# A hyena, mLSTM and S5 block on one core: the S5 output tables move from the first stage to the scan, the late modulation takes one k and 1024 columns per operation

## The chip, the cores and the metric

The kernel runs on one NeuronCore of a Trainium2 chip. The time is the device time of one execution in microseconds (us); the figure for the kernel before is the median of three runs.

## The reference

One layer of a hybrid diffusion block on 256 latent tokens that follow 256 context tokens, 2048 channels wide, all in fp32. An adaLN modulation is made from `c` and `c_ctx` (a 2048 x 12288 product). The modulated tokens go through one input projection (2048 x 12304), whose columns feed three branches of 768 channels: a two-step Hyena long convolution, a bidirectional mLSTM and a bidirectional S5 state space model. Each branch is projected to 2048, multiplied with a sigmoid gate per channel (also columns of the input projection), the sum goes through an output projection, a norm and a squared-ReLU MLP of width 8192.

```python
def token_mixer(h_ctx, h_lat, rows, need_ctx, w_in, hy_p, ml_p, s5_p, out_p):
    ...
    ys_c, sst_f, sst_b = s5_bidir(u_c, disc, c_re, c_im, zs, zs, need_ctx)
    ys_l, _, _ = s5_bidir(u_l, disc, c_re, c_im, sst_f, sst_b, True)
    y_lat = merge_branches(hyena_branch(hy_l, rows, *hy_p), mlstm_out(hm_l, o_l, ml_norm_g),
                           s5_out(ys_l, u_l, s5_d, glu_w, glu_b), mg_l, *out_p)

def s5_direction(u, ab_re, ab_im, bb_re, bb_im, c_re, c_im, x0, readout):
    ...
    _, _, s_re, s_im = lax.associative_scan(s5_combine, (a_re, a_im, bu_re, bu_im), axis=1)
    ...
    y = (jnp.einsum('blgp,gcp->blgc', s_re, c_re.astype(F32))
         - jnp.einsum('blgp,gcp->blgc', s_im, c_im.astype(F32)))
    return y, final
```

## The kernel before

Every weight matrix is streamed once, in chunks of 128 x 1024 fp32 (512 KB) that `raw` (L196) loads on SP's queue into four buffers `wr`. For fp32 precision each chunk is split in two parts: ACT copies it to `wh` (L190), DVE subtracts to `wl` (L194), and three matmuls per tile (L211) multiply the parts with the split activations. So each chunk costs one ACT and one DVE operation of 128 x 1024 and, with 256 tokens moving, 24 matmuls.

Each engine has one stream of instructions in a fixed order, which a scheduler made from the program's order and priorities; an engine whose next instruction waits holds up all behind it, DMA issues included (SP, ACT and GpSimd, here POOL, issue DMAs). Work other than the chunks is written as generators, *sides*: after each chunk `chunk_done` (L216) advances up to three of them, each by its rate, and `drain` runs one to its end. The stages in `run` (L1407 to L1536):

- *Stage 0* (scope p0a). The first 4096 columns of the modulation: 8 blocks of 16 chunks, each a fp32 matmul (L406), whose sums end in `modc` (L415). After each pair of blocks `h_group` (L427) multiplies and shifts a quarter of the tokens' channels (L435, on DVE) and splits them, and a quarter of the K projection follows (`part`). Beside it, one step per chunk, runs the side `s5_params` (L440: discretised powers of the poles, `pq`, and the scaled input matrix `s5B`) and `s5_tables` (L540).
- `s5_tables` makes, for six channel tiles, products of powers with C (the output tables Q, lines L536 to L538 in `powers`, L525) and with B (the input tables w). Direction 0 is computed on DVE, direction 1 on POOL. Q goes to DRAM as QD (L568) and, by small matmuls (`pk`, L564), becomes the near-diagonal kernel KK; w is transposed and goes to DRAM as WA.
- *pA.* `s5_spread` (L598) rearranges KK into KD by 8 DMAs; a small gate on kT makes it wait for K. Then V, gates, Q, the mLSTM, U (`u_consume`, L600, which writes UD and keeps the latent u in SBUF as `uT`) and O. The rest of the modulation, `mod_late` (L1164), is a side: 16 blocks of 512 columns, 8 loads of two k rows each, one DVE multiply-add of 128 x 512 (L1181) for each k.
- *pB.* Six chunks of the hyena columns, then `s5_inject` (L616: WA and u, loaded on ACT's queue, give the 64 chunk inputs of the state), then the side `s5_scan` (L645): 63 steps that depend on each other, each of four POOL operations of 128 x 96 (L652 to L655). Beside it the remaining hyena chunks and 32 gate chunks (`mg_consume`, which writes gates to DRAM, MG). Then the side `s5_output` (L658), which needs the scan's end and loads QD, KD and UD on ACT's queue, beside 48 more gate chunks, and `s5_glu`.
- *pC.* `hyena` (L1096), the last 16 of 96 gate chunks, the merges, and the tail: output projection, norm, MLP.

`hy_consume` (L1078) convolves three taps on DVE (L741, L743) and writes HX on POOL's queue (L1087, L1094).

## Time and profile before

| | us |
| --- | --- |
| three runs | 2031.83, 2034.3, 2036.18 |
| median | 2034.3 |
| the profiled execution | 2046.25 |
| its span | 2044.3 |

| engine | busy us | share of the span | instructions |
| --- | --- | --- | --- |
| PE | 1885.0 | 92% | 13945 |
| DVE | 1342.6 | 66% | 1842 |
| ACT | 797.7 | 39% | 1079 |
| POOL | 473.4 | 23% | 654 |

The DMA engines moved 455.92 MB in the span, 223 GB/s on average. Busy shares are averages over stages with different limits, so the rows further down are cut by stage: up to 205 us the last `modc` sum, from 634 to 807 us the scan. The times of rows are of the profiled execution, which is 12 us above the median.

### The profile page before, as it was taken

The numbers are of one execution on the slowest core, as the hardware profiler recorded it, in microseconds if no ns is written. First come the engines' busy times: TensorE is split into PE (matmuls) and PEld (weight loads), VectorE is DVE, ScalarE is ACT, GpSimd is POOL, SyncE is SP. The second block draws the span as 40 slices with busy tenths as digits, with TensorE's granted clock in tenths as the row PEclk, the third lists the DMA queues.
The fourth block names the chain that finished last, engine by engine and source line by source line (L and its number), as shares of the span: only waits on it lengthen the run. The fifth ranks groups of instructions, "written<-read, shape, count | busy, mean of one in ns | idle before, by whom it ended". The sixth has DMA issues, their size and how long they took to land.

```text
span 2044.3 us, 34693 instructions
## 1 busy us (share of the span) xinstructions
PE 1885.0 (92%) x13945; PEld 1716.5 (84%) x13945; DVE 1342.6 (66%) x1842; ACT 797.7 (39%) x1079; POOL 473.4 (23%) x654
## 2 busy tenths in 40 slices
PE   4787899999999896999889998899999999999996
PEld 1555888898998896999769977899989899998986
DVE  8789876655876564455777767866655555555556
ACT  1233333324544332534333443544343334444332
POOL 4777311000015997000343400500000000000001
PEclk8898899999999898999999999999999999999998
DMA  8798667766698675777756876577765566666653
GB/s 311 262 299 285 195 203 221 228 199 184 206 318 272 211 242 172 262 251 243 270 183 217 278 249 218 174 248 229 244 208 190 189 185 181 184 185 230 190 187 115
DMA packets 255200, 455.92 MB, mean 223 GB/s; under 512 B 28789, under 2 KB 75541, under 8 KB 253504
## 3 DMA queue, kind: packets, MB, share of 16 engines
q1 hardware_dynamic: 221824, 382.43, 59.0%
q0 software_dynamic: 12384, 44.54, 6.2%
q10 hardware_dynamic: 20832, 26.75, 3.9%
q8 instruction: 109, 1.79, 0.4%
q14 instruction: 51, 0.42, 0.1%
HBM read 424.75 MB, written 32.05 MB: 223 GB/s over the span
## 4 chain that ended last, share of the span: by engine, by line
PE 64%; DVE 14%; DMA 8%; POOL 8%; issue 4%; ACT 1%; ACTq 0%; POOLq 0%; DVEq 0%; SPq 0%
PE mm L211 57%; DMA wr<-in_w_mod_dram 4%; PE aux L211 4%; DVE wl L194 4%; POOL sc L654 2%; POOL sc L653 2%; POOL t L655 2%; POOL sc L652 2%; DVE t L194 1%; DMA wr<-in_w_in_dram 1%; DVE ty L435 1%; ACT wh L190 1%; DVE mac L1181 1%; DVE s5t L537 1%; DMA s5wq<-WA 1%
## 5 line engine op out<-in xcount | busy, mean ns | idle before, releaser
L211 PE MATMUL mm<-t,wh 128*128 128x256 f32 x5888 | 1102.7, 288 | 24.8 <-ACT wh L190 12.6
L211 PEld LDWEIGHTS mm<-t,wh 128*128 128x128 f32 x5888 | 933.7, 194 | 46.6 <-ACT wh L190 13.9
L194 DVE TENSOR_TENSOR wl<-wr,wh 128x1024 fp32r<-128x1024 f32 (+1 forms) x517 | 657.0, 1277 | 381.6 <-ACT wh L190 380.7
L211 PE MATMUL mm<-t,wl 128*128 128x256 f32 x2944 | 850.1, 289 | 23.3 <-DVE wl L194 23.0
L190 ACT ACTIVATE wh<-wr 128x1024 fp32r<-128x1024 f32 (+1 forms) x517 | 546.4, 1058 | 807.9 <-PE mm L211 577.6
L211 PEld LDWEIGHTS mm<-t,wl 128*128 128x128 f32 x2944 | 571.4, 194 | 37.4 <-DVE wl L194 29.4
L1181 DVE SCALAR_TENSOR_TENSOR mac<-wr,vecs,mac 128x512 f32<-128x512 f32 x240 | 186.8, 778 | 152.7 <-DMA wr<-in_w_mod_dram 150.0
L211 PE MATMUL mm<-wh,t 128*128 128x512 f32 (+1 forms) x960 | 249.3, 349 | 1.7 <-ACT wh L190 1.7
L211 PEld LDWEIGHTS mm<-wh,t 128*128 128x128 f32 x960 | 169.7, 191 | 25.6 <-ACT wh L190 2.7
L211 PE MATMUL mm<-wl,t 128*128 128x512 f32 (+1 forms) x480 | 169.2, 352 | 5.2 <-DVE wl L194 5.2
L211 PE MATMUL mm<-wh,ff 128*128 128x512 f32 (+1 forms) x576 | 155.3, 358 | 0.0
L211 PEld LDWEIGHTS mm<-wh,ff 128*128 128x128 f32 x576 | 101.8, 188 | 17.6
L211 PEld LDWEIGHTS mm<-wl,t 128*128 128x128 f32 x480 | 91.6, 191 | 21.7 <-DVE wl L194 10.5
L211 PE MATMUL mm<-wl,ff 128*128 128x512 f32 (+1 forms) x288 | 103.0, 357 | 0.0
L1403 POOL DMA_DIRECT2D t<-in_ln_g_dram x1 | 0.5, 535 | 358.8 <-PE mm L211 358.8
L211 PE MATMUL mm<-ty,wh 128*128 128x256 f32 x384 | 74.1, 291 | 0.0
L211 PE MATMUL mm<-ty,wl 128*128 128x256 f32 x192 | 57.0, 297 | 6.7 <-DVE wl L194 6.7
L211 PEld LDWEIGHTS mm<-ty,wh 128*128 128x128 f32 x384 | 61.6, 195 | 0.9
L211 PEld LDWEIGHTS mm<-wl,ff 128*128 128x128 f32 x288 | 54.2, 188 | 8.8
L1192 POOL DMA_DIRECT2D mrow<-b x8 | 4.0, 502 | 227.8 <-DVE b L1190 227.8
L211 PE MATMUL aux<-t,t 128*128 128x384 f32 (+3 forms) x160 | 48.8, 422 | 8.0 <-DVE t L1147 3.5
L406 PE MATMUL px<-wr,b 128*32 128x512 f32 x128 | 40.3, 714 | 12.9 <-DVE s5t L335 10.7
(389 smaller groups left out, 1813.6 us busy)
## 6 DMA issues: line engine op xcount, KB each, us to landing
wr<-in_w_ff_dram SPq DMA_DIRECT2D x256, 512.0 KB, 3.9
wr<-in_w_in_dram SPq DMA_DIRECT2D x192, 512.0 KB, 4.7
wr<-in_w_mod_dram SPq DMA_DIRECT2D x160, 512.0 KB, 4.8
wr<-in_w_out_dram SPq DMA_DIRECT2D x32, 512.0 KB, 4.9
wh<-in_w_mod_dram SPq DMA_DIRECT2D x16, 512.0 KB, 6.2
wl<-in_w_mod_dram SPq DMA_DIRECT2D x16, 512.0 KB, 7.8
QD<-s5Q POOLq DMA_DIRECT2D x24, 256.0 KB, 4.9
WA<-s5wa ACTq DMA_DIRECT2D x24, 256.0 KB, 5.2
```

The lines of the kernel that those rows point to most:

```text
L190: return self.nc.scalar.activation(out, in_, f, bias=bias, scale=scale)
L194: self.nc.vector.tensor_sub(lo, x, hi.bitcast(F32))
L211: self.nc.tensor.matmul(out, lhsT, rhs, start=start, stop=stop, skip_group_check=True)
L406: nc.tensor.matmul(ps[o:o + 32], self.st[:, k, :], raw[:, kk, :], start=k < 4, stop=k >= KT - 4, skip_group_check=True, tile_position=(0, o))
L435: self.nc.vector.tensor_scalar(h[:, j], h[:, j], self.modc[:, 16 + k, m:m + 1], self.modc[:, k, m:m + 1], op0=ALU.mult, op1=ALU.add)
L537: e.tensor_mul(t[:, :, s], bcp(s), bcm(1))
L652: v.tensor_mul(t1, self.a8[:, 0], S[:, :, :, :, n - 1])
L653: v.tensor_mul(t2, self.a8[:, 1], S[:, :, ::-1, :, n - 1])
L654: v.tensor_add(t1, t1, S[:, :, :, :, n])
L655: v.tensor_add(S[:, :, :, :, n], t1, t2)
L1181: v.scalar_tensor_tensor(acc, x, c, acc, op0=ALU.mult, op1=ALU.add)
L1192: nc.gpsimd.dma_start(self.mrow[which // 3:which // 3 + 1, o:o + 512], brow)
```

## The change

1. `h_group`'s multiply and shift goes from DVE to ACT.
2. `s5_tables` is split. `s5_into` stays in stage 0 and makes the input tables alone, for both directions on DVE and four pairs per operation (128 x 512 and 128 x 1024 elements where there were 128 x 256 and 128 x 512); it saves `s5B` and `pq` to DRAM (SB, PQ). The output tables, `pk`, QD and KK are a side (rate 0.6) in a new scope pT, from the end of the injection on, beside hyena and gate columns; they load SB, PQ and C anew, all products on DVE (128 x 576 and 128 x 1152). QD and KK are written on ACT's queue. `s5_spread` comes at their end, and the gate on K is gone.
3. `s5_inject` starts after four hyena chunks where there were six, and loads WA in 24 pieces of 256 KB, on POOL's queue.
4. `uT` goes through DRAM (UL). `s5_output` loads all it needs on POOL's queue, at rate 0.4 beside 24 gate chunks; 40 gate chunks in place of 16 are left for beside and behind hyena.
5. `mod_late` loads one k and 1024 columns at a time, with one DVE operation of 128 x 1024 for each load, 128 loads of 512 KB as before.
6. The mLSTM's states take four smaller tiles in place of one large one.

```diff
-                    self.nc.vector.tensor_scalar(h[:, j], h[:, j], self.modc[:, 16 + k, m:m + 1],
-                                                 self.modc[:, k, m:m + 1], op0=ALU.mult, op1=ALU.add)
+                    self.act(h[:, j], h[:, j], AF.Identity, bias=self.modc[:, k, m:m + 1],
+                             scale=self.modc[:, 16 + k, m:m + 1])
...
-    def powers(self, out, m, d, q, l0, n):
+    def powers(self, out, m, d, ct, l0, n):
-        e = self.nc.vector if d == 0 else self.nc.gpsimd
-        k = q.stop - q.start
+        v = self.nc.vector
+        q = slice(24 * d + 4 * ct, 24 * d + 4 * ct + 4)
...
         for s in range(2):
-            e.tensor_mul(out[:, :, s], bcp(1 + s), bcm(0))
-            e.tensor_mul(t[:, :, s], bcp(s), bcm(1))
-        e.tensor_add(out, out, t)
+            v.tensor_mul(out[:, s], bcp(1 + s), bcm(0))
+            v.tensor_mul(t[:, s], bcp(s), bcm(1))
+        v.tensor_add(out, out, t)
+
+    def s5_into(self):
+        nc = self.nc
+        for ct in range(CT):
+            wt = []
+            for d in range(2):
+                w = self.t(self.br, [P, 2, 4, P], "s5w", 4)
+                self.powers(w.rearrange("p s q (l c) -> p s q l c", c=16), self.s5B, d, ct, d, LC)
+                wt.append(w)
+            yield
...
     def s5_tables(self):
...
+        nc.gpsimd.dma_start(B.rearrange("p a b c -> p (a b c)"), self.SB)
+        nc.gpsimd.dma_start(self.pq.rearrange("p a b c -> p (a b c)"), self.PQ)
+        nc.gpsimd.dma_start(C, self.I["s5c"])
+        yield
         for ct in range(CT):
...
+            for d in range(2):
+                q = slice(24 * d + 4 * ct, 24 * d + 4 * ct + 4)
+                Q = self.t(self.br, [P, 2, 4, 144], "s5Q", 2)
+                self.powers(Q.rearrange("p s q (l c) -> p s q l c", c=16), C, d, ct, 0, 9)
...
-                    nc.gpsimd.dma_start(self.QD[ct, d, :, 2 * half:2 * half + 2], Q[:, :, :, o:o + P])
+                nc.scalar.dma_start(self.QD[ct, d], Q[:, :, :, o:o + P])
...
+        self.s5_spread()
...
     def s5_inject(self):
...
-            wa = self.t(self.br, [P, 4, 4, P], "s5wq", 2)
-            nc.scalar.dma_start(wa, self.WA[ct])
...
+            for i in range(4):
+                wa = self.t(self.br, [P, 4, P], "s5wa", 4)
+                nc.gpsimd.dma_start(wa, self.WA[ct, :, i])
...
-        for b in range(16):
-            c0 = 2 * D + b * 512
-            acc = self.t(self.sm, [P, 512], "mac", 1)
-            for k0 in range(0, KT, 2):
-                wt = self.raw(w, k0, 2, c0, 512)
...
+        for b in range(8):
+            c0 = 2 * D + b * 1024
+            acc = self.t(self.sm, [P, 1024], "mac", 1)
+            for k in range(KT):
+                x, c = self.raw(w, k, 1, c0, 1024)[:, 0], self.sc[:, k:k + 1]
...
-                    yield from self.s5_tables()
+                    yield from self.s5_into()
...
-            with self.scope("pB") as self.br:
-                self.n6 = 5
-                hy = self.lin_w_steps(w_in, O_HY, 3 * W, KT, lat, self.hy_consume)
-                self.run_steps(hy, 6)
-                self.s5_inject()
+            hy = self.lin_w_steps(w_in, O_HY, 3 * W, KT, lat, self.hy_consume)
+            with self.scope("pT") as self.br:
+                self.run_steps(hy, 4)
+                for _ in self.s5_inject():
+                    pass
                 self.sides[1][1] = 0.3
                 self.with_side(self.s5_scan(), 2)
+                self.with_side(self.s5_tables(), 0.6, 2)
                 self.run_steps(hy, 36)
-                self.run_steps(steps, 32)
-                self.with_side(self.s5_output(), 0.6)
-                self.run_steps(steps, 48)
+                self.run_steps(steps, 24)
+                self.drain(2)
+            with self.scope("pB") as self.br:
+                self.run_steps(steps, 8)
+                self.with_side(self.s5_output(), 0.4)
+                self.run_steps(steps, 24)
                 self.drain()
                 self.s5_glu()
```

How the change moves instructions is shown at three places. First DVE late in stage 0, around two `modc` sums of the kernel before (`s5t` and `s5Q` are the table products, `s5w` the input tables, `ty` sums of K):

```order
L537 TENSOR_TENSOR s5t_31_129<-s5pq_189,s5B_121 128x2x128 x2
L538 TENSOR_TENSOR s5w_1325<-s5w_1325,s5t_31_129 128x512
L537 TENSOR_TENSOR s5t_31_129<-s5pq_189,s5C_122 128x2x144 x2
L536 TENSOR_TENSOR s5w_1470<-s5pq_189,s5B_121 128x2x128 x2
L1460 TENSOR_TENSOR ty_108<-ty_108,mm_1758 128x1024
L590 TENSOR_TENSOR s5kk_1408<-s5kk_1408,aux_1152 128x16
L536 TENSOR_TENSOR s5w_1596<-s5pq_189,s5B_121 128x2x128 x2
L194 TENSOR_TENSOR wl_1843<-wr_1840,wh_1842 128x1024
L415 TENSOR_TENSOR modc_101<-px_1820,vecs_93 128x8
L536 TENSOR_TENSOR s5Q_216_1419<-s5pq_189,s5C_122 128x2x144 x2
```

and DVE at a like place of the kernel after:

```order
L537 TENSOR_TENSOR s5w_722<-s5pq_190,s5B_124 128x512 x2
L194 TENSOR_TENSOR t_23_106<-ty_113,t_23_106 128x512
L539 TENSOR_TENSOR s5w_716<-s5w_716,s5t_130 128x1024
L194 TENSOR_TENSOR wl_979<-wr_976,wh_978 128x1024
L538 TENSOR_TENSOR s5t_130<-s5pq_190,s5B_124 128x512 x2
L539 TENSOR_TENSOR s5w_722<-s5w_722,s5t_130 128x1024
L1476 TENSOR_TENSOR ty_110<-ty_110,mm_899 128x1024
L194 TENSOR_TENSOR wl_1060<-wr_1057,wh_1059 128x1024
L1476 TENSOR_TENSOR ty_111<-ty_111,mm_975 128x1024
L415 TENSOR_TENSOR modc_104<-px_1037,vecs_96 128x8
```

The products with C (`s5Q`, 128x2x144) are gone from the stage; those with B (`s5w`) come in one operation for four pairs, and stand earlier.

Second, POOL late in the scan. Before, the four operations of a step (`sc`, `t`) with a gate write (MG) now and then:

```order
L652 TENSOR_TENSOR sc_850_6418<-t_713_5520 128x96
L653 TENSOR_TENSOR sc_851_6419<-t_713_5520 128x96
L654 TENSOR_TENSOR sc_850_6418<-sc_850_6418,t_713_5520 128x96
L655 TENSOR_TENSOR t_713_5520<-sc_850_6418,sc_851_6419 128x96
L1211 DMA MG_74<-mg_7562 128x512
L652 TENSOR_TENSOR sc_852_6424<-t_713_5520 128x96
L653 TENSOR_TENSOR sc_853_6425<-t_713_5520 128x96
L1211 DMA MG_74<-mg_7565 128x512
L654 TENSOR_TENSOR sc_852_6424<-sc_852_6424,t_713_5520 128x96
```

and after, with hyena writes (HX), gate writes, the eight DMAs of `s5_spread` (KD) and two loads of `s5_output` (QD) inside one step of the scan, whose four lines are L666 to L669 now:

```order
L666 TENSOR_TENSOR sc_901_6359<-t_637_4883 128x96
L667 TENSOR_TENSOR sc_902_6360<-t_637_4883 128x96
L1102 DMA HX_93<-b_999_6937 128x256
L1102 DMA HX_93<-b_1000_6942 128x256
L680 MEMSET b_1146_8192 128x1024
L668 TENSOR_TENSOR sc_901_6359<-sc_901_6359,t_637_4883 128x96
L1224 DMA MG_74<-mg_7545 128x512
L1224 DMA MG_74<-mg_7548 128x512
L611 DMA KD_73<-KK_92 48x16x128 x8
L686 DMA s5wq_8198<-QD_77 128x2x1024
L686 DMA s5wq_8316<-QD_77 128x2x1024
L669 TENSOR_TENSOR t_637_4883<-sc_901_6359,sc_902_6360 128x96
```

All these DMAs now stand in the stream that carries the scan: 37 between its first and its last step, with 10 memsets, where there were 15 and 2.

Third, DVE beside the scan. Before, the splits of the weight chunks (`wl`), the multiply-adds of `mod_late` (`mac`) and the convolution of hyena (`b`):

```order
L1181 SCALAR_TENSOR_TENSOR mac_6472<-wr_7398,vecs_93,mac_6472 128x512
L194 TENSOR_TENSOR wl_7335<-wr_7332,wh_7334 128x1024
L1181 SCALAR_TENSOR_TENSOR mac_6472<-wr_7398,vecs_93,mac_6472 128x512
L194 TENSOR_TENSOR wl_7371<-wr_7368,wh_7370 128x1024
L741 SCALAR_TENSOR_TENSOR b_1008_7279<-b_1007_7277,vecs_93,b_1008_7279 128x4x63
L741 SCALAR_TENSOR_TENSOR b_1009_7284<-b_1007_7277,vecs_93,b_1009_7284 128x4x63
L743 SCALAR_TENSOR_TENSOR b_1008_7279<-b_1007_7277,vecs_93,b_1008_7279 128x4x63
L743 SCALAR_TENSOR_TENSOR b_1009_7284<-b_1007_7277,vecs_93,b_1009_7284 128x4x63
L194 TENSOR_TENSOR wl_7405<-wr_7402,wh_7404 128x1024
```

and after:

```order
L539 TENSOR_TENSOR s5Q_5845<-s5Q_5845,s5t_5320 128x1152
L194 TENSOR_TENSOR wl_6381<-wr_6378,wh_6380 128x1024
L759 SCALAR_TENSOR_TENSOR b_810_5869<-b_806_5857,vecs_96,b_810_5869 128x4x63
L538 TENSOR_TENSOR s5t_5320<-s5pq_5319,s5C_5318 128x576 x2
L194 TENSOR_TENSOR wl_6432<-wr_6429,wh_6431 128x1024
L194 TENSOR_TENSOR wl_6477<-wr_6474,wh_6476 128x1024
L537 TENSOR_TENSOR s5Q_6366<-s5pq_5319,s5C_5318 128x576 x2
L539 TENSOR_TENSOR s5Q_6080<-s5Q_6080,s5t_5320 128x1152
L757 SCALAR_TENSOR_TENSOR b_813_5879<-b_806_5857,vecs_96,b_813_5879 128x4x63
L194 TENSOR_TENSOR wl_6531<-wr_6528,wh_6530 128x1024
L538 TENSOR_TENSOR s5t_5320<-s5pq_5319,s5C_5318 128x576 x2
```

The products and sums of the output tables (`s5Q`, `s5t`) and of KK stand between the splits. From the injection to the first operation that needs the scan's end, DVE has 143 operations where it had 88: 48 splits (44 before), 13 multiply-adds of 1024 (26 of 512), 26 of the convolution (14), 38 table products of 128 x 576 and 10 table sums of 128 x 1152 (none), and small ones.

## Rows read from the trace of the kernel before

**Rows 1.** Windows: length; busy (count) of PE, PEld, DVE, ACT, POOL; clock; DMA; GB/s.

```profile
0.00:40.00 40.00, 19.60 (x82) 4.48 (x82) 32.48 (x134) 5.41 (x18) 11.54 (x30) 0.87 0.95 343
40.00:100.00 60.00, 43.72 (x304) 31.43 (x306) 47.18 (x57) 18.47 (x50) 48.05 (x58) 0.80 0.75 251
100.00:180.00 80.00, 63.12 (x477) 45.50 (x472) 71.08 (x86) 26.17 (x75) 58.00 (x75) 0.89 0.91 298
...
0.00:205.00 205.00, 146.51 (x1024) 95.64 (x1024) 173.37 (x299) 59.20 (x165) 137.57 (x189) 0.88 0.86 290
```

**Rows 2.** DVE's groups to 205 us: xcount | busy us, mean ns | idle us.

```profile
L536 DVE TENSOR_TENSOR s5Q<-s5pq,s5C 128x288 f32<-128x288 f32 x24 | 19.2, 838 | 6.1 <-PE aux L564 6.1
L537 DVE TENSOR_TENSOR s5t<-s5pq,s5C 128x288 f32<-128x288 f32 x24 | 18.9, 822 | 0.2
...
L435 DVE TENSOR_SCALAR ty<-ty,modc 128x256 f32<-128x256 f32 x24 | 16.9, 772 | 0.1
L538 DVE TENSOR_TENSOR s5w<-s5w,s5t 128x512 f32<-128x512 f32 x11 | 16.5, 1498 | 0.3
```

**Rows 3.** POOL's issues of QD in the same stretch, columns as rows 2.

```profile
L568 POOL DMA_DIRECT2D QD<-s5Q x23 | 18.0, 783 | 13.9 <-DVE s5Q L538 11.7 <-POOL s5Q L538 1.8 <-POOL s5bb L554 0.3
```

**Rows 4.** DVE's timeline behind the last modc sum: start us, length us.

```profile
204.99 0.16 DVE L415 TENSOR_TENSOR modc<-px,vecs 128x8 f32<-128x8 f32 x1
205.07 3.12 DVE L537 TENSOR_TENSOR s5t<-s5pq,s5B 128x256 f32<-128x256 f32 x2
208.11 4.63 DVE L435 TENSOR_SCALAR ty<-ty,modc 128x256 f32<-128x256 f32 x8
```

**Rows 5.** ACT's timeline there, one operation of 128 x 256.

```profile
213.62 0.42 ACT L190 ACTIVATE b<-b 128x256 fp32r<-128x256 f32 x1
```

**Rows 6.** Chain of waits where PE runs without a stop: start, length.

```profile
418.37 34.63 PE mm L211 x287
```

**Rows 7.** Window of the scan, columns as rows 1.

```profile
634.00:807.00 173.00, 141.52 (x1118) 138.90 (x1116) 93.74 (x93) 57.08 (x66) 162.62 (x267) 0.92 0.67 216
```

**Rows 8.** Groups in the scan's window, columns as rows 2.

```profile
L194 DVE TENSOR_TENSOR wl<-wr,wh 128x1024 fp32r<-128x1024 f32 x45 | 63.4, 1433 | 20.0 <-ACT wh L190 20.0
L1181 DVE SCALAR_TENSOR_TENSOR mac<-wr,vecs,mac 128x512 f32<-128x512 f32 x26 | 23.8, 914 | 28.9 <-DMA wr<-in_w_mod_dram 28.7
L1211 POOL DMA_DIRECT2D MG<-mg x8 | 4.6, 573 | 0.1
L743 DVE SCALAR_TENSOR_TENSOR b<-b,vecs,b 128x252 f32<-128x252 f32 x7 | 4.4, 657 | 0.0
...
L666 POOL MEMSET b<- 128x1024 f32 x1 | 1.0, 966 | 0.0
```

**Rows 9.** Tile sc, the scan's first operation: ns min/median/max, first to last start us.

```profile
L652 POOL TENSOR_TENSOR sc<-t x63: 433/446/1302, 634.4 to 806.8; 128x96 f32<-128x96 f32 x63
```

**Rows 10.** POOL's timeline at the scan's end: one step to the next.

```profile
799.72 0.43 POOL L652 TENSOR_TENSOR sc<-t 128x96 f32<-128x96 f32 x1
...
801.49 0.44 POOL L652 TENSOR_TENSOR sc<-t 128x96 f32<-128x96 f32 x1
```

**Rows 11.** What PE waited for at L687, the first output matmuls: us, times.

```profile
POOL sc L652: 31.8, 2
```

**Rows 12.** DVE's groups from 300 to 600 us, columns as rows 2.

```profile
L194 DVE TENSOR_TENSOR wl<-wr,wh 128x1024 fp32r<-128x1024 f32 x62 | 75.5, 1221 | 35.8 <-ACT wh L190 35.5
L1181 DVE SCALAR_TENSOR_TENSOR mac<-wr,vecs,mac 128x512 f32<-128x512 f32 x83 | 62.1, 748 | 24.3 <-DMA wr<-in_w_mod_dram 23.1
...
L935 DVE TENSOR_TENSOR DT<-DT,t 128x512 f32<-128x512 f32 x14 | 9.5, 687 | 2.4 <-ACT DT L190 2.3
```

**Rows 13.** Window of hyena, columns as rows 1.

```profile
960.00:1110.00 150.00, 131.56 (x950) 121.18 (x949) 115.79 (x144) 54.74 (x77) 55.08 (x57) 0.95 0.67 222
```

**Rows 14.** DMA issues on the page: KB each, median us to landing.

```profile
s5wq<-WA ACTq DMA_DIRECT2D x6, 1024.0 KB, 10.2
```

More of the change, by code (lines that the diff above doesn't have):

```diff
@@ L445, in s5_params @@
         nc.gpsimd.dma_start(par, I["s5a"])
-        B, C = (self.t(self.br, [P, 2, 48, 16], tag, 1) for tag in ("s5B", "s5C"))
+        B = self.t(self.br, [P, 2, 48, 16], "s5B", 1)
         nc.gpsimd.dma_start(B, I["s5b"])
-        nc.gpsimd.dma_start(C, I["s5c"])
         yield
         are, aim, lg = par[:, 0, :], par[:, 1, :], par[:, 2, :]
-        self.work = [self.t(self.br, [P, 1152], f"s5t{d}", 1) for d in range(2)]
-        tmp = self.slices(self.work[0][:, :1104].rearrange("p (a n) -> p a n", n=48))
+        self.work = self.t(self.br, [P, 1152], "s5t", 1)
+        tmp = self.slices(self.t(self.br, [P, 23, 48], "s5tmp", 1))
         dt_, mag, ph, cs, sn = (tmp(x) for x in ("dt", "mag", "ph", "cs", "sn"))
@@ L503, in s5_params @@
         br, bi = B[:, 0], B[:, 1]
-        w1, w2 = (self.work[1][:, 384 * i:384 * i + 384].rearrange("p (q c) -> p q c", c=16) for i in range(2))
+        w1, w2 = (self.work[:, 384 * i:384 * i + 384].rearrange("p (q c) -> p q c", c=16) for i in range(2))
         for d in range(2):
@@ new lines, in s5_tables @@
+            for d in range(2):
+                q = slice(24 * d + 4 * ct, 24 * d + 4 * ct + 4)
+                Q = self.t(self.br, [P, 2, 4, 144], "s5Q", 2)
+                self.powers(Q.rearrange("p s q (l c) -> p s q l c", c=16), C, d, ct, 0, 9)
+                bb = self.t(self.br, [P, 2, 4, 32], "s5bb", 2)
+                nc.gpsimd.memset(bb, 0.0)
+                for h in range(2):
+                    for s in range(2):
+                        self.act(bb[64 * h:64 * h + 64, s, :, 16 * h:16 * h + 16],
+                                 B[64 * h:64 * h + 64, s, q, :], scale=1.0 - 2.0 * s)
+                yield
+                l0 = 0 if d == 0 else 16
+                for s in range(2):
+                    for p in range(4):
+                        nc.tensor.matmul(pk[32 * p:32 * p + 32, d, :], bb[:, s, p, :], Q[:, s, p, l0:l0 + P],
+                                         start=d == 0 and s == 0, stop=s == 1, skip_group_check=True,
+                                         tile_position=(0, 32 * p))
+                o = 16 - l0
+                nc.scalar.dma_start(self.QD[ct, d], Q[:, :, :, o:o + P])
@@ L687, in s5_output @@
                         self.nc.tensor.matmul(py[o:o + 64, p // 2, :], xb[:, p, d, s].rearrange("p g j -> p (g j)"),
-                                              Q[:, d, p, s, :], start=p < 2 and d == 0 and s == 0, stop=False,
+                                              Q[:, d, s, p, :], start=p < 2 and d == 0 and s == 0, stop=False,
                                               skip_group_check=True, tile_position=(0, o))
@@ L1169, in mod_late @@
         w = self.I["w_mod"][0]
-        for b in range(16):
-            c0 = 2 * D + b * 512
-            acc = self.t(self.sm, [P, 512], "mac", 1)
-            for k0 in range(0, KT, 2):
-                wt = self.raw(w, k0, 2, c0, 512)
-                for kk in range(2):
-                    k = k0 + kk
-                    x, c = wt[:, kk], self.sc[:, k:k + 1]
-                    if k == 0:
-                        v.tensor_scalar(acc, x, c, None, op0=ALU.mult)
-                    else:
-                        v.scalar_tensor_tensor(acc, x, c, acc, op0=ALU.mult, op1=ALU.add)
-                if k0 + 2 < KT:
+        for b in range(8):
[3 more added lines that the diff above has]
+                x, c = self.raw(w, k, 1, c0, 1024)[:, 0], self.sc[:, k:k + 1]
+                if k == 0:
+                    v.tensor_scalar(acc, x, c, None, op0=ALU.mult)
+                else:
+                    v.scalar_tensor_tensor(acc, x, c, acc, op0=ALU.mult, op1=ALU.add)
+                if k + 1 < KT:
@@ L1183, in mod_late @@
                     yield
-            which = b // 4
+            which, o = divmod(b, 2)
+            o *= 1024
             if which in (0, 3):
-                ps = self.aux([1, 512], "px")
-                self.mm(ps, self.ones, acc, True, True)
-                brow = self.b2([1, 512])
-                nc.gpsimd.dma_start(brow, self.I["b_mod"][0:1, c0:c0 + 512])
-                v.tensor_add(brow, brow, ps)
-                o = (b % 4) * 512
-                nc.gpsimd.dma_start(self.mrow[which // 3:which // 3 + 1, o:o + 512], brow)
-            else:
-                ps = self.aux([P, 4], "px")
-                for j in range(4):
+                brow = self.b4([1, 1024])
+                nc.gpsimd.dma_start(brow, self.I["b_mod"][0:1, c0:c0 + 1024])
+                for i in range(0, 1024, 512):
+                    ps = self.aux([1, 512], "px")
+                    self.mm(ps, self.ones, acc[:, i:i + 512], True, True)
+                    v.tensor_add(brow[:, i:i + 512], brow[:, i:i + 512], ps)
+                nc.gpsimd.dma_start(self.mrow[which // 3:which // 3 + 1, o:o + 1024], brow)
+            else:
+                ps = self.aux([P, 8], "px")
+                for j in range(8):
```

126 lines of the change are left out of this document (52 added, 74 removed).

## The prediction, blind

> **What bounds the kernel now.** PE is busy 92% of the span, so what matters is where it is not, and I read the windows by stage first. Up to 205 us PE works 146.5 us of 205; DVE is at 85% and the DMA engines at a share of 0.86 [rows 1]. The stage is bound by weights that must arrive, and held below full DMA pace by DVE, which has the S5 tables between the splits: in the first 40 us, where few tables are made, the share is 0.95, then 0.75 and 0.91. The other large hole is the scan: from 634 to 807 us PE works 141.5 of 173 us [rows 7], and the wait is at its end, where the first output matmuls stood 31.8 us until POOL was done [rows 11]. So the scan's length on POOL sets that stretch.
>
> Why is it so long? At its end, where nothing else runs, a step takes 1.77 us [rows 10], so 63 steps would take 111.5 us. From 634.4 to 806.8 us they take 172.4, and single operations whose median is 446 ns take up to 1302 [rows 9]. 15 DMA issues at 0.57 us [rows 8] and two memsets of about 1 us are 11 of the difference. The other 50 us came beside 93.74 us of busy DVE [rows 7]: each microsecond of DVE work costs the scan 0.53 us. That is my price for everything DVE is given in this stretch.
>
> **The change part by part.** All sums are against the profiled execution (2046.25 us); the forecast is the same difference from the median, 2034.3.
>
> *Stage 0.* Removed: 24 and 24 products with C on DVE at 0.84 and 0.82 us, as many on POOL, and the writes of QD [rows 2, 3]. L435's 24 operations of 0.77 us go to ACT, whose operations of that shape take 0.42 [rows 5] and which is at 29%. Added: DVE makes the input tables of both directions, 24 and 24 products of 512 elements and 12 sums of 1024; at 1.50 us for 512 elements [rows 2] the products are 72 us, half of which DVE had before. DVE thus loses some 40 + 17 us and gains 36, and POOL, which slows it, has nearly nothing left. Bytes: the window moves 290 GB/s x 205 us = 59.4 MB in 176 us of full DMA work (0.86 x 205). QD and C take 6.8 MB with them, of which 1.45 (SB, PQ) and about 1 MB of WA, now all within the stage, come back: 4.4 MB x 2.97 us = 13 us, leaving 163, and I add 3 us for the smaller packets of those writes: 166 us. At which share? Between 0.86 as now (193 us, a gain of 12) and 1.0 (166 us, a gain of 39) I take 0.92, nearest to the 0.91 and 0.95 of the stretches that run well: 180 us, a gain of 25. Behind the last `modc` sum stood 3.12 us of table products and 4.63 us of L435 before the next split [rows 4]; L435 costs ACT 8 x 0.42 = 3.4 us. That gives 5. **Stage 0: -30** (-12 to -46, the upper end with all 7.75 us).
>
> *Start of the scan.* With four hyena chunks ahead in place of six, and side work set otherwise, 120 fewer matmuls of 256 columns stand between V and the scan. At 34.63/287 = 0.1207 us [rows 6]: **-14.5**. They aren't saved, they come later.
>
> *The scan.* DVE work beside it, from the order: 48 splits x 1.433 = 69 us; 13 multiply-adds of 1024, each 0.748 plus 512 elements at the slope of 1221 against 687 ns, 1.28 us, slowed as the splits are (1433 against 1221, x 1.2), 1.54 us, together 20; 26 convolutions x 0.657 = 17 [rows 8, 12]; 38 table products of 576 at 687 ns x 576/512 x 1.2 = 0.93, 35 us; 10 sums of 1152 at 1.6, 16 us; small ones 2. Sum 159 us, x 0.53 = 84. To this 37 DMA issues x 0.6 = 22 us and 10 memsets, 4 us. So 111.5 + 84 + 22 + 4 = 221.5 us against 172.4: **+49**. Lower bound: tables at their free time (43 us, 23 after x 0.53), eight more us for convolutions, issues that hide in gaps: +31. Upper bound: tables at the 1.50 us per 512 elements that products took beside a busy POOL, 87 us, 46 after x 0.53; with 8, 24 for issues and memsets and some 5 where a DMA waits for its data in POOL's stream (KD for the last KK): +83. PE can fill 1188 x 0.1207 = 143 us and some 20 for `pk` and small ones of the 221; it stands about 58 us at the first output matmuls. What would hide the scan's length is more chunks, and those stand behind.
>
> The Trainium skill (SBUF — State Buffer, Who interferes with whom) says that a DVE operation with two SBUF inputs contends with a GpSimd one that reads SBUF, and that the loser blocks for the whole instruction; by it each microsecond of such DVE work would cost the scan one, and the rival of the full lock below is this rule's result. The trace agrees that they contend, but at 0.53 us for each.
>
> *After the scan.* 7890 matmuls where there were 7825: 65 x 0.1207 = **+7.8**. Hyena has 24 more gate chunks to lie beside. PE works 131.6 of 150 us there [rows 13]; I take a quarter of those 18 us back, **-5** (-15 to +5: DVE is at 77% there, and the chunks bring it splits).
>
> *The late modulation.* The same 128 loads; a 1024 operation in place of two of 512 saves the fixed part, 687 - 512 x (1221 - 687)/512 = 0.15 us [rows 12], 18 us of DVE over the 120 pairs. DVE isn't what PE waits for in most of the kernel: **-2** (-4 to 0).
>
> *Injection.* WA comes in 24 pieces through four buffers on POOL's queue: five refills. 1 MB took 10.2 us [rows 14], so 51 us, against 390 matmuls x 0.1207 = 47 us between the first and the last injection. I take 0, bounds 0 to +15 (each refill 3 us late). `uT` through DRAM: six writes on ACT's queue and six loads hidden beside chunks, 0. The mLSTM's four tiles: 0.
>
> **Sum:** -30 - 14.5 + 49 + 7.8 - 5 - 2 = **+5.3, about 2040 us**.
>
> **The rivals.**
>
> *Faster.* Stage 0 runs at full DMA pace and the tables cost the scan little: -44 - 14.5 + 40 + 7.8 - 5 - 2 = -17.7, 2017 us. For it speak the share of 0.95 in the first 40 us and the DVE time that stage 0 loses; against it that the K chunks and DVE's splits stay, and that the share was 0.91 at best later. It decides if the last `modc` sum comes before 172 us and the scan takes under 215. Chance 0.34.
>
> *The loads on POOL's queue bind.* Injection starts 3 us late at each refill, +15: 2055 us. For it: four buffers of 256 KB, a queue that carries other loads. Against: the first four are loaded long before. Chance 0.14.
>
> *A full lock.* Each microsecond of two-input DVE work stops the scan for one: 48 x 1.22 + 13 x 1.28 + 17 + 43 = 135 us at free durations, 111.5 + 135 + 26 = 273 us, +100 in place of +49: 2091 us. Against it: the same count on the scan of before, 45 x 1.22 + 26 x 0.75 + 9 = 84, would make it 206 us, and it took 172.4. Chance 0.06.
>
> *The change doesn't do what it says.* The order shows the tables beside the scan, not behind it: their last sum stands two thirds of the way to the first operation that needs the scan's end. So "beside hyena and gate columns" is beside the scan, which is my forecast itself.
>
> **How the numbers follow.** A measurement can tell about 0.2%, 4 us, from no change. The forecast (0.46) by its own spread, 2024 to 2058, gives slower 0.34, same 0.09, faster 0.03; the faster rival gives faster 0.33 and same 0.01; the queue slower 0.13, same 0.01; the lock slower 0.06. Together faster 0.36, same 0.11, slower 0.53. Below, the range goes to 2006 (all of stage 0 and the scan at +31 give -28.7); above to 2074 (the scan's upper bound, +34 more). What lies outside is the lock and the ends of both cases, under 0.2.
>
> **What would show it right or wrong.** Right: the last `modc` sum at about 180 us; the scan at 215 to 228 us from first to last step, 3.5 us a step; POOL's operations at 0.7 us mean beside DVE; a wait of about 58 us for POOL at the first output matmul; PE's busy time unchanged. Wrong: a scan under 200 us, which would say that products with broadcast inputs cost POOL less than splits do; a `modc` sum still at 195 us, which would say that stage 0 was never held by tables; PE waiting for `s5wa` before the scan.

## The result and the profile after

The changed kernel takes 2056.69 us (four runs, 2049.97 to 2061.03) against 2033.16 for the kernel before (four runs): a ratio of 1.0111 with a 95% interval of 1.0077 to 1.0144, some 23 us slower. A second set of four runs, beside the last experiments, gave 1.0113 (1.0076 to 1.0149). The forecast was 2040 us, slower, with a range of 2006 to 2074.

To see where the time went I cut both traces at the same five places: the last of the 64 gate matmuls that follow V's first chunks, the scan's first step, the first output matmul, the first transpose of x in the tail, the end. First the kernel before, windows by these cuts (columns as in [rows 1]):

```profile
0.00:242.30 242.30, 176.35 (x1250) 123.75 (x1251) 204.99 (x348) 73.97 (x188) 146.93 (x205) 0.87 0.82 274
242.30:634.40 392.10, 387.99 (x3216) 361.05 (x3215) 268.39 (x530) 156.42 (x252) 33.24 (x50) 1.00 0.72 226
634.40:807.60 173.20, 141.12 (x1114) 138.50 (x1113) 93.93 (x92) 57.67 (x68) 163.19 (x268) 0.92 0.67 215
807.60:1280.30 472.70, 439.08 (x3340) 408.37 (x3340) 318.65 (x396) 198.14 (x257) 95.45 (x104) 0.97 0.73 242
1280.30:2044.00 763.70, 740.49 (x5030) 684.79 (x5030) 456.59 (x480) 311.51 (x317) 34.59 (x30) 0.98 0.62 195
```

and the changed kernel, by the same cuts:

```profile
0.00:203.20 203.20, 159.80 (x1058) 113.20 (x1059) 121.38 (x246) 69.15 (x112) 9.17 (x33) 0.88 0.88 300
203.20:600.10 396.90, 379.68 (x3090) 350.31 (x3089) 253.11 (x467) 148.04 (x251) 35.09 (x67) 0.97 0.66 209
600.10:824.00 223.90, 167.11 (x1361) 158.83 (x1360) 146.68 (x145) 73.26 (x126) 203.45 (x298) 0.89 0.70 225
824.00:1300.40 476.40, 442.36 (x3411) 414.57 (x3411) 316.12 (x362) 199.52 (x260) 106.44 (x118) 0.98 0.75 244
1300.40:2057.00 756.60, 736.42 (x5032) 681.24 (x5032) 455.07 (x462) 311.47 (x317) 35.29 (x28) 0.99 0.63 198
```

Read the second number of each line (length) and the third (PE busy). The first cut comes 39.1 us earlier, with DVE busy 121 us where it was 205 and POOL 9 where it was 147. The stretch up to the scan is 4.8 us longer though PE has 8.3 us less to do in it. The scan's stretch is 50.7 us longer, the next 3.7, the tail 7 shorter. PE's work is the same in both (1885 us), so the time is its idle time: 66.0, 4.1, 32.1, 33.6 and 23.2 us before; 43.4, 17.2, 56.8, 34.0 and 20.2 after. Of the scan's 50.7 us, 26.0 are work of PE that now lies there. In idle time stage 0 gives 22.6 us back, and the start of the scan (13.1) and the scan (24.7) take more than that.

These stages sum to +13 us, not to the 23 of the medians: the profiled execution of before lies 12 us above its median, that of the changed kernel 3. A second profile of the kernel before (e8, span 2041.0) has 246.3, 388.7, 175.0, 472.1 and 758.9 us, so a stage of one profile is good to about 5 us. Against the second profile of the changed kernel (e12) the difference is 18.5 us.

Stage 0 ran as the first rival, "Faster", asked (its other condition, a scan under 215 us, was not met): the last `modc` sum came at 170.21 us, where it was 204.99 [rows 4], and the window before it (columns as in [rows 1]) has the DMA share at 0.92, the value that the forecast took:

```profile
0.00:170.00 170.00, 132.58 (x848) 86.69 (x848) 97.36 (x212) 52.59 (x86) 6.96 (x29) 0.89 0.92 315
```

The scan: tile sc in the changed kernel, to be held against [rows 9] (433 ns at the least, 446 at the median; from first to last start 223.0 us where it was 172.4):

```profile
L666 POOL TENSOR_TENSOR sc<-t x63: 428/498/2172, 600.1 to 823.1; 128x96 f32<-128x96 f32 x63
```

DVE's groups beside it, the changed kernel from 600 to 824 us, against [rows 8]:

```profile
L194 DVE TENSOR_TENSOR wl<-wr,wh 128x1024 fp32r<-128x1024 f32 x48 | 64.4, 1346 | 49.8 <-ACT wh L190 47.4 <-PE mm L211 2.2
...
L537 DVE TENSOR_TENSOR s5Q<-s5pq,s5C 128x576 f32<-128x576 f32 x19 | 19.2, 1047 | 3.0 <-PE aux L591 3.0
L1193 DVE SCALAR_TENSOR_TENSOR mac<-wr,vecs,mac 128x1024 f32<-128x1024 f32 x13 | 18.2, 1398 | 4.2 <-DMA wr<-in_w_mod_dram 4.1
L538 DVE TENSOR_TENSOR s5t<-s5pq,s5C 128x576 f32<-128x576 f32 x18 | 18.0, 1037 | 0.0
L539 DVE TENSOR_TENSOR s5Q<-s5Q,s5t 128x1152 f32<-128x1152 f32 x10 | 15.8, 1575 | 0.0
```

The table operations are there, 53 us. But DVE's splits idled 47.4 us for ACT, and the waits of the same stretch (us, times, longest) tell why:

```profile
ACT s5bb L190 <- POOL s5bb L581: 65.4, 8, 12.0
...
PE mm L211 <- ACT wh L190: 25.5, 8, 9.1
...
ACT b L190 <- POOL t L669: 17.1, 1, 17.1
ACT b L190 <- DMA HX<-b: 15.3, 3, 10.6
PEld aux L703 <- POOL sc L666: 14.1, 1, 14.1
...
PE mm L211 <- DVE wl L194: 9.5, 14, 1.6
```

ACT, whose queue also holds the splits `wh`, waited 65.4 us for the eight zeroings of `s5bb` (0.3 us each) that stand in POOL's stream between steps of the scan. So PE was held up along the whole stretch, and at its end only 14 us were left of the 58 us that the forecast put there.

### The profile page after: what moved, and what is told of

Its sections match the earlier page's. It is cut to its first block, busy times and chain, and to the rows that moved or that the text cites. A ratio compares the mean times of both kernels' runs of the same rounds, so it can differ in the third digit from the quotient of the medians.

```text
span 2057.8 us, 34431 instructions
## 1 busy us (share of the span) xinstructions
PE 1885.4 (92%) x13945; PEld 1718.2 (83%) x13945; DVE 1292.4 (63%) x1678; ACT 801.4 (39%) x1062; POOL 389.4 (19%) x540
## 5 line engine op out<-in xcount | busy, mean ns | idle before, releaser
L211 PE MATMUL mm<-t,wh 128*128 128x256 f32 x5888 | 1117.9, 290 | 58.0 <-ACT wh L190 33.6
L194 DVE TENSOR_TENSOR wl<-wr,wh 128x1024 fp32r<-128x1024 f32 x517 | 651.0, 1262 | 488.9 <-ACT wh L190 480.9
L190 ACT ACTIVATE wh<-wr 128x1024 fp32r<-128x1024 f32 x517 | 545.0, 1057 | 804.2 <-PE mm L211 585.5
L1193 DVE SCALAR_TENSOR_TENSOR mac<-wr,vecs,mac 128x1024 f32<-128x1024 f32 x120 | 162.1, 1350 | 114.4 <-DMA wr<-in_w_mod_dram 113.8
L211 PE MATMUL mm<-ty,wh 128*128 128x256 f32 x384 | 68.3, 280 | 0.6 <-ACT wh L190 0.6
```

Source lines behind the costliest of these rows:

```text
L190: return self.nc.scalar.activation(out, in_, f, bias=bias, scale=scale)
L194: self.nc.vector.tensor_sub(lo, x, hi.bitcast(F32))
L211: self.nc.tensor.matmul(out, lhsT, rhs, start=start, stop=stop, skip_group_check=True)
L1193: v.scalar_tensor_tensor(acc, x, c, acc, op0=ALU.mult, op1=ALU.add)
```

## The experiments

Every ratio is to the kernel before, run beside on the same chip. Theory A: the scan's length on POOL, 0.53 us for each us of DVE work, sets the stretch. Later, as A2: PE is starved by ACT, held in POOL's stream; and to remove that is worth something only if there are chunks to put before the scan's end.

**e1.** The zeroing of `s5bb` on DVE.

```diff
-                nc.gpsimd.memset(bb, 0.0)
+                v.memset(bb, 0.0)
```

> The changed kernel with one edit: the zeroing of the small tiles s5bb (L581) is done by DVE, not by POOL. In the changed kernel's trace ACT, whose queue also holds the splits, waited 65.4 us for these eight memsets, which stand in POOL's stream between steps of the scan. Theory A, the scan's own length sets the stretch (224 us from its first step to the first output matmul): the idle time of PE only moves from the middle to the end, the wait for POOL at the first output matmul grows from 14 to about 50 us, the scan stays at 217 to 225 us, and the time stays within 5 us of the changed kernel's, ratio to before 1.008 to 1.013. Rival B, these waits are what is lost: PE gets back most of the 43 us that it idled before the end, the time falls by 20 us or more, ratio about 1.000 or under.

Measured: 2050.14 us, ratio 1.0072 (1.0051 to 1.0093), a little below A's range and the changed kernel's interval, though the two intervals overlap. The scan took 215.5 us. Rival B is out: the waits went, 20 us did not come back. But A was wrong on where the idle time goes. It stayed in the middle, PE standing only 4 us at the output, because the next dependence took over. The waits of e1 from 596.5 to 813 us:

```profile
ACT b L190 <- DMA HX<-b: 50.9, 6, 11.7
```

The buffers of `hy_consume` come free behind the HX writes, which POOL issues, and these too stand between the scan's steps.

**e2.** No products of the output tables (Q one tile of zeros).

```diff
-                Q = self.t(self.br, [P, 2, 4, 144], "s5Q", 2)
-                self.powers(Q.rearrange("p s q (l c) -> p s q l c", c=16), C, d, ct, 0, 9)
+                Q = Q0
```

> The changed kernel without the products of the output tables: Q is one tile of zeros, and the 24 + 24 products of 128 x 576 and 12 sums of 128 x 1152 on DVE are left out (the S5 output then lacks the scan's part); memsets, small matmuls, all DMAs stay. Theory A (0.53 us of scan for each us of DVE work beside it): 53 us of DVE work leave the scan's stretch, which falls by 28 us to about 196 us, and the time by about 25 us, ratio to before about 0.999. Rival C, it is the DMA issues and memsets in POOL's stream that lengthen the scan: the scan stays over 212 us and the time falls by under 10 us, ratio 1.007 or more. A full lock between DVE and POOL would take 45 us or more off the scan.

Measured: 2041.31 us, ratio 1.0025 (1.0007 to 1.0042). The scan took 199.2 us, where A said 196 and C over 212; DVE's work beside it fell from 147.4 to 104.5 us only, since other work filled part of the 53; a full lock, a microsecond for each, would have taken the scan to about 180. The time fell by 15 to 18 us rather than 25; in this profile the stretch before the scan was 10 us longer (407 us). So the products beside the scan are worth most of the 23 us, but without them the kernel is still not faster than before.

**e3.** e1 and sixteen more gate chunks ahead of the output.

```diff
-                self.run_steps(steps, 8)
+                self.run_steps(steps, 24)
                 self.with_side(self.s5_output(), 0.4)
```

> The kernel of e1 (memsets on DVE) and sixteen more gate chunks ahead of the S5 output: 24 + 24 where 24 + 8 stood, so that 24 are left for beside and behind hyena in place of 40. Theory A: PE idles about 50 us for the scan's end, and sixteen chunks are 16 x 24 x 0.12 = 46 us of matmuls to fill it; they bring 16 splits, which cost the scan 16 x 1.35 x 0.53 = 11 us. So PE's wait at the first output matmul falls to under 20 us and the time by 25 to 35 us against the changed kernel, less up to 10 for hyena with less beside it: ratio to before 0.995 to 1.003. Rival D, chunks beside hyena are worth as much as chunks beside the scan: the time changes by under 8 us, ratio 1.007 to 1.014.

Measured: 2055.18 us, ratio 1.0097 (1.0071 to 1.0122), in rival D's range. Yet it tells nothing of D: the scheduler put the first output matmul behind 1180 matmuls of the chunks, just as in e1, and spread the output over the added chunks. The edit did not do what it says. To hold the output back takes a dependence of data (e6).

**e4.** HX, MG and KD written on ACT's queue.

```diff
-            self.nc.gpsimd.dma_start(self.MG[ct0 // 4][:, h:h + 2], t)
+            self.nc.scalar.dma_start(self.MG[ct0 // 4][:, h:h + 2], t)
```

(and the same for the two writes of HX and the eight of KD)

> The changed kernel with the writes HX, MG and KD (about 30 of the 37 DMAs in the scan) issued on ACT's queue in place of POOL's. Theory A: each takes 0.57 to 0.74 us of POOL's time and nothing else of the scan, together some 19 us, so the scan falls from 223 to about 204 us and the time by 15 to 20 us, ratio to before 1.002 to 1.004. Rival E, ACT's queue is the worse place, since the splits wait behind a DMA that waits for its data: PE's waits for wh grow, the time falls by under 8 us or rises, ratio 1.007 or more.

Measured: 2055.12 us, ratio 1.0101 (1.0067 to 1.0135), where A had said 1.002 to 1.004, and so in rival E's range; but the scan took 189.6 us, 33 less. Much of both goes back to what stood before the first output matmul: 961 matmuls in place of 1196. With 12% less DVE work in it and without the issues the scan is shorter, and the chunks that no longer lie beside it lie behind. Over its five stretches PE idled 15 us less than in the changed kernel and was busy 12 us longer, which leaves little of it. PE's waits for `wh` were 29.1 us, not far from the 25.5 of the changed kernel, and E's mechanism is tested better by e5, where they are 6.5 with the same queue. PE idled 44.7 of the 191.2 us, and ACT waited for the memsets still (waits of e4, 598.5 to 789.7 us):

```profile
ACT s5bb L190 <- POOL s5bb L581: 72.0, 8, 11.7
```

**e5.** Both edits, e1 and e4.

> The changed kernel with both edits of the runs before together: the memsets of s5bb on DVE, and HX, MG and KD written on ACT's queue. In e1 ACT then waited 51 us for HX writes (their buffers come free when POOL, inside the scan, issues the write), in e4 72 us for the memsets; each edit alone left the other. Theory A2: what starves PE in the middle of the scan's stretch is ACT, which also splits the weight chunks, held by instructions in POOL's stream; with both gone PE no longer idles in the middle (waits for wh and wl together under 15 us, after 39 and 35 in e4 and e1), and all its idle time, 45 to 60 us, is one wait for POOL at the first output matmul, since only 939 matmuls stand ahead of it; the scan takes 180 to 192 us; the time is as in e1 and e4, ratio to before 1.004 to 1.011. Rival F, PE is starved by DVE's load or the weight loads: the idle time stays spread over the stretch and the wait at the output stays under 15 us.

Measured: 2055.36 us, ratio 1.0081 (1.0066 to 1.0096), as A2 said. The scan took 189.9 us. The waits of e5 from 596.2 to 787 us: one wait at the output, a little under the 45 us expected, and 12.5 us for the splits, so F is out as what holds PE most.

```profile
ACT b L190 <- POOL t L669: 45.5, 1, 45.5
PE aux L703 <- ACT b L190: 41.7, 1, 41.7
...
PE mm L211 <- ACT wh L190: 6.5, 1, 6.5
PE mm L211 <- DVE wl L194: 6.0, 7, 2.0
```

F's engine is close to its limit there, though: in the first 123.8 us DVE was busy 119.95 us (third busy time of the line), and PE idled 10.9.

```profile
596.20:720.00 123.80, 112.94 (x990) 107.08 (x990) 119.95 (x133) 57.20 (x110) 119.07 (x123) 0.97 0.80 246
```

**e6.** e5, and the output held back by data until a gate of the 40th gate chunk is there.

```diff
-                self.run_steps(steps, 8)
+                self.run_steps(steps, 16)
+                self.nc.vector.scalar_tensor_tensor(self.sign, self.mg_last[:, 0, 0:2], 0.0, self.sign,
+                                                    op0=ALU.mult, op1=ALU.add)
                 self.with_side(self.s5_output(), 0.4)
...
-                    self.act(xb[r, :, 0, s, h, :], self.S[r, 0, s, pr, 31:63], scale=1.0 - 2.0 * s)
+                    self.act(xb[r, :, 0, s, h, :], self.S[r, 0, s, pr, 31:63], scale=self.sign[r, s:s + 1])
```

> The kernel of e5, and the S5 output held back by data (the sign that its operands are multiplied with is made from a gate of the 40th gate chunk), so that 1369 matmuls of 256 columns stand between the injection and the first output matmul, where the changed kernel has 1196, e5 939. Theory A2: 1369 x 0.1207 + some 20 us of other PE work are 185 us, about the length of the scan of 185 to 200 us; PE's idle time in that stretch falls from 57 us (changed kernel) to under 20, and the time by 25 to 40 us against the changed kernel: ratio to before 0.990 to 0.999. Rival D, what lies beside the scan lacks beside hyena afterwards: PE's idle time there grows by as much, ratio 1.004 or more.

Measured: 2026.83 us, ratio 0.9942 (0.9922 to 0.9963): faster than both kernels, and 1.4% faster than e5, from which it differs by this one edit. The scan is hardly shorter than in e1 (211.8 us against 215.5, where 185 to 200 had been expected), but PE has work beside it. Windows of e6 (columns as in [rows 1]), the scan's stretch and the one behind it:

```profile
598.80:811.70 212.90, 182.91 (x1545) 176.24 (x1545) 160.17 (x167) 83.40 (x141) 203.39 (x259) 0.94 0.82 256
811.70:1269.50 457.80, 423.74 (x3237) 394.47 (x3237) 303.03 (x353) 193.30 (x252) 99.16 (x103) 0.97 0.74 246
```

PE idles 30.0 us there (56.8 in the changed kernel; A2 had said under 20), and no more behind it (34.1 against 34.0), so D is out.

**e7.** The changed kernel with the late modulation of before.

> The changed kernel with the late modulation of the kernel before (two k and 512 columns per load, 240 multiply-adds of 512). Prediction's term: the 1024 form saves 0.15 us of DVE a pair and 2 us of time (0 to 4), so the ratio to before is that of the changed kernel, 1.011, plus 0 to 0.002. Rival G, the 1024 form costs: a multiply-add of 1.28 to 1.40 us stands in front of a split where one of 0.75 did, and PE's 15 us of stalls between V and the scan are partly this; then the ratio falls to 1.006 or less.

Measured: 2069.66 us, ratio 1.0155 (1.0137 to 1.0172). This lies above what the prediction's term allows. The 1024 form is worth about 9 us by the ratios, though the intervals overlap, so the size is uncertain; G's ratio is out. All multiply-adds of e7 and of the changed kernel, DVE's groups over the whole run:

```profile
L1196 DVE SCALAR_TENSOR_TENSOR mac<-wr,vecs,mac 128x512 f32<-128x512 f32 x240 | 189.9, 791 | 101.7 <-DMA wr<-in_w_mod_dram 98.8
```

```profile
L1193 DVE SCALAR_TENSOR_TENSOR mac<-wr,vecs,mac 128x1024 f32<-128x1024 f32 x120 | 162.1, 1350 | 114.4 <-DMA wr<-in_w_mod_dram 113.8
```

28 us of DVE, not 18. The stretch from the first cut to the scan, though, was shorter in e7: 381.3 us, PE idle 6.6. So most of the stalls before the scan (below) seem to come with the 1024 form, which is G's other half, and it earns more than that behind: e7's three later stretches are 9.9, 6.8 and 3.7 us longer. It isn't the scan that is longer; from first to last start it took 214.4 us, less than the changed kernel's 223.0:

```profile
L666 POOL TENSOR_TENSOR sc<-t x63: 428/491/1518, 589.2 to 803.6; 128x96 f32<-128x96 f32 x63
```

Nor does PE wait more: over the five stretches it idled 172.0 us (171.6 in the changed kernel) and was busy 1894.5 us (1885.4). Why the 512 form costs is open.

**e8.** The kernel before again.

> The kernel before, once more, for a second profile: the profiled execution read ahead of the change lies 12 us above the median of its runs. Expected: ratio 0.998 to 1.002, a span of about 2030 to 2036 us in the profile, and the 10 us in one stage: either stage 0 (last modc sum near 197 rather than 205 us) or spread over all of them.

Measured: ratio 0.9992 (0.9975 to 1.0010), span 2041.0, above the 2030 to 2036 expected; the last `modc` sum at 208.6 us. The difference to the first profile is spread over the stages.

**e9.** The kernel before with its output held back in the way of e6 (48 and 32 gate chunks where 32 and 48 were).

> The kernel before with one edit: its S5 output is held back by data as in e6 (behind 48 gate chunks in place of 32), so that 1421 matmuls of 256 columns stand between the injection and the first output matmul, where it had 1141. Theory A2: in the kernel before, PE idles 32 us in the scan's stretch; 1421 x 0.1207 = 172 us and some 6 of other PE work cover a scan that the 12 added splits lengthen to about 182 us; PE's idle time there falls to 8 to 15 us and the time by 12 to 24 us, ratio 0.988 to 0.994, no worse than e6. Rival H, the move of the tables is worth its 39 us in stage 0 as soon as the scan is covered: then this kernel gains less than e6, ratio 0.996 to 1.000.

Measured: 2027.46 us, ratio 0.9954 (0.9936 to 0.9973), between the two forecasts, with an interval that reaches into both. The scan took 182.4 us, as said. PE idled 18.4 us in the stretch, 1421 matmuls being more than it needs: the output came some 10 us behind the scan's end. It is level with e6, the intervals overlapping: with the scan covered in both, all the rest of the change, with the edits of e1 and e4, shows no gain. What the moved tables bring by themselves isn't shown by this, since e6 also has L435 on ACT (e11) and the 1024 form (e7).

**e10.** e6 with the output tables begun beside U and O.

> The kernel of e6 with the side of the output tables begun earlier, beside the U and O projections (rate 0.8; the mLSTM's result lies in another buffer for room), and 1501 matmuls between the injection and the first output matmul. Theory A2: about half of the table products leave the scan's stretch for one where POOL is idle, 25 us of DVE work x 0.53 = 13 us less of scan for the same other work; ratio to before 0.986 to 0.993. Rival I, DVE becomes the bound beside U and O (it was busy 48 of 76 us there): what the scan saves is lost between V and the scan, ratio 0.994 or more.

Measured: 2033.73 us, ratio 0.9982 (0.9961 to 1.0004): rival I's range. The scan fell to 187.4 us, but PE idled 29.0 of the 447.7 us ahead of it (15.7 of 393.0 in e6), and its output came 24 us behind the scan's end. But the profiled execution, 2026.56 us, is one of the fastest of the ten and level with e6, so its trace doesn't show where the 7 us of the medians went.

**e11.** The kernel before with L435's work on ACT, nothing else.

> The kernel before with the modulation of the tokens (L435) on ACT alone, all tables where they were. Prediction's term: stage 0 gains up to 5 us behind the last modc sum and little before it, ratio 0.996 to 0.999. If the whole gain of stage 0 came from this edit and not from the tables, the last modc sum would come before 185 us; the theory says 198 to 206 us.

Measured: 2024.79 us, ratio 0.9950 (0.9930 to 0.9971), the lowest median of all and level with e6 and e9. The last `modc` sum came at 198.2 us, as said, 7 to 10 us earlier than in the two profiles of before, where "little" had been expected ahead of it. The first cut came at 232.6 us, 10 to 14 us earlier (window as in [rows 1], against 242.3 and 246.3 us):

```profile
0.00:232.60 232.60, 174.74 (x1250) 123.85 (x1251) 180.95 (x315) 88.02 (x220) 145.71 (x206) 0.85 0.85 285
```

**e12.** The changed kernel again.

> The changed kernel once more, beside the others on one chip. Expected: a ratio within 1.0077 to 1.0144, PE idle 50 to 60 us in the scan's stretch, ACT waiting 55 to 75 us for the memsets of s5bb.

Measured: 2060.58 us, ratio 1.0113 (1.0076 to 1.0149). Idle 56.9 us in the scan's stretch, ACT's wait for the memsets 66.7 us, all as expected.

## Why the prediction was right, and where not

**The sign and the main term: right.** Stage 0's gain is outweighed by the scan's stretch, +50.7 us in the traces where +49 was forecast. That it came so close is partly luck: DVE had 147 us of work beside the scan and not 159, which is 6 us less of scan, while POOL waited 13.6 us for others, for which the sum had nothing (5 in its upper bound). The price of 0.53 us of scan per us of DVE work, worked out from the scan of before, holds roughly in the others once these waits, read from the traces afterwards, are added. Scan from first step to last, against 111.5 + 0.53 x DVE + 0.6 x issues + what POOL waited for others:

| kernel | DVE busy | issues | POOL waits | formula | measured |
| --- | --- | --- | --- | --- | --- |
| before | 95.0 | 16 | 4.1 | 175.6 | 174.3 |
| changed | 147.4 | 38 | 13.6 | 226.0 | 224.9 |
| e2, no products | 104.5 | 37 | 7.7 | 196.8 | 201.1 |
| e5, uncoupled | 128.2 | 6 | 10.0 | 193.1 | 191.8 |
| e6, covered | 160.6 | 6 | 10.0 | 210.2 | 213.6 |
| e9, before covered | 107.5 | 16 | 4.1 | 182.2 | 184.2 |

(A window reaches one step past the last start. Memsets, 2 to 5 us, are not counted. Of the eight runs that the table leaves out six lie within 5 us of the formula; e4 took 191.5 us against 183.9, e7 215.8 against 221.8.) So the rival of the full lock is out: in e2, where 43 us of DVE work went, the scan lost 24. The rule it came from (the Trainium skill, SBUF — State Buffer, Who interferes with whom) has the loser block for the whole instruction. How that goes together with a price of about half is open; no run here shows for which part of DVE's time POOL was held.

**Stage 0, -30: mis-sized.** The traces show -39.1, inside its bounds and near the first rival's -44: 34.8 up to the last `modc` sum, where 25 was forecast, and 4.3 behind it, where it was 5. The DMA share was 0.92 as taken, but 0.92 x 170 us are 156 us of full DMA work where the count had come to 166, 3 of them for small packets, which no run shows. And the prediction gave DVE too much: 1.50 us for a product of 512 elements, the time that a sum of that size took beside a busy POOL [rows 2]. With POOL nearly idle such products took 0.69 us, 31 us in all where 72 were counted, and the splits 1223 ns where they had taken 1525 (DVE's groups to the first cut, the changed kernel, then the kernel before):

```profile
L194 DVE TENSOR_TENSOR wl<-wr,wh 128x1024 fp32r<-128x1024 f32 x15 | 18.3, 1223 | 19.4 <-ACT wh L190 17.7 <-DMA WA<-s5wa 1.6
L538 DVE TENSOR_TENSOR s5t<-s5pq,s5B 128x512 f32<-128x512 f32 x24 | 15.5, 689 | 0.2
L537 DVE TENSOR_TENSOR s5w<-s5pq,s5B 128x512 f32<-128x512 f32 x24 | 15.1, 688 | 14.8 <-PE aux L214 14.8
```

```profile
L194 DVE TENSOR_TENSOR wl<-wr,wh 128x1024 fp32r<-128x1024 f32 x15 | 22.9, 1525 | 0.0
```

e11 tells that 10 to 14 us come from L435's move alone if the tables stay, which the prediction had at the 5 us behind the last `modc` sum: the likely reason is that on DVE these operations stood in the way in each quarter, not only in the last (not tried apart).

**Start of the scan, -14.5: the step that failed.** The traces show +4.8. PE's work there fell by 8.3 us (126 matmuls fewer, at a granted clock of 0.97 where it was 1.00), but its idle time rose from 4.1 to 17.2: a gap of some 7 us between Q and the mLSTM, where PE waited for DVE's convolution (6.4 us at L759 in one piece), and 7 us in the injection. The prediction priced matmuls and not what lies between them. e7 has -10.8 and 6.6 us of idle time there, so most of the gaps seem to come with the new rhythm of the late modulation, which e7 undoes. The loads on POOL's queue, the second rival, didn't bind: none of PE's waits in the injection was for `s5wa`.

**PE stands 58 us at the first output matmul: right in amount, wrong in place.** It idled 56.8 us in the stretch, 14 of them there. The place was misread already for the kernel before: the 31.8 us of [rows 11] add up one wait, of PE and of its weight loads. PE stood 15.8 us at the output, and 16 of its 32 us of idle time lay ahead of that, in waits for splits (waits of before, 634.4 to 808.7 us):

```profile
PEld aux L687 <- POOL sc L652: 16.0, 1, 16.0
PE aux L687 <- POOL sc L652: 15.8, 1, 15.8
...
PE mm L211 <- ACT wh L190: 9.2, 2, 6.0
...
PE mm L211 <- DVE wl L194: 7.0, 8, 1.4
```

The prediction counted the memsets and the HX and MG writes at their time on POOL and did not ask who waits for them. e1, e4 and e5 show the answer one by one, and that it cost nothing of itself: free of both, PE ran ahead and waited 41.7 us in one piece.

**After the scan, +7.8 - 5 = +2.8: right** (+3.7). **Late modulation, -2: mis-sized**, about -9 by e7, with overlapping intervals and the cause open.

**The total, +5.3, measured +23.** In the first pair of traces the stages come to +13; stage 0 gave 9 us more than forecast, the start of the scan 19 less, and the tail gave 7 that no term has. The second pair, e12 less e8, has -42.0, +5.9, +50.0, +4.9 and -0.3, together +18.5: the tail's 7 us came from the first profile of before (763.7 us, where e8, e9 and e11 have 758 to 759) and not from the change. The rest lies between profiles and medians, and I can't place it. That the sign came out is in part luck: it hung on a sum of +5.3 with errors of 9 one way and 19 the other, and the prediction gave slower a chance of 0.53.

**What the cause is.** The change lengthens the scan by 50 us and puts only 26 us more of PE's work before its end. The table products are about half of that lengthening (24 us in e2), and without them 15 to 18 of the 23 us are gone. But what they cost hangs on whether the scan is covered: e6, which differs from e5 in the output held back alone, takes PE's idle time over the five stretches from 169.9 to 143.4 us and is 1.4% faster than e5, 1.7% faster than the changed kernel, with all the products beside the scan. e9 shows that the kernel before gains from the same edit (0.5%). The 13 us of idle time at the start of the scan are a second part of the loss, and e6 keeps most of them (15.7 us idle there). Whether e11's edit and e9's add up was not tried.

## What to carry to other kernels

When work is moved beside a serial chain, price its effect on the chain, and then ask how many microseconds of other work the scheduler has really put ahead of the chain's consumer; placing the code later does not move it, a dependence does. Any small operation (a zeroing, a DMA issue) that is put into the chain's engine hands that engine's pace to whoever waits for it: look down the waits for an engine that holds the main loop's work. And price edits that ride along alone: here the smallest of them was a gain that the rest hid.

## What the runs showed that I had not expected

A memset of 0.3 us held ACT for up to 12.0 us, because it stood between operations of the scan; eight of them, 65 us. Engines with time to spare (in that stretch of 223.9 us ACT was busy 73 us, DVE 147) can thus be tied to one that has little (POOL, 203).

PE's granted clock followed its idle time. The scan's stretch in e5, where PE idled 59.6 us, and in e9, where it idled 18.4 (columns as in [rows 1], the clock is the third number from the end):

```profile
596.20:787.00 190.80, 131.24 (x1117) 124.69 (x1117) 127.28 (x141) 63.27 (x120) 181.29 (x257) 0.85 0.68 211
```

```profile
633.80:828.50 194.70, 176.28 (x1396) 173.17 (x1395) 112.80 (x108) 72.59 (x85) 178.05 (x274) 0.96 0.73 232
```

The means of 0.85 and 0.96 are mixtures of the full clock (2.4 GHz) and the half (1.2 GHz); from 745 to 787 us of e5, where PE did 0.3 us of work, the mean is 0.54, and ahead of the scan, where PE hardly idles, the kernel before has 1.00. PE's busy time isn't quite a constant either: 1877.9 us in e11, 1889.4 in e12 and 1897.2 in e4, for about the same work. How much of that is the clock the runs don't show, but a spread of 19 us is as large as most effects here, so a change in idle time alone does not give the change in time.
